# Retention's matrix work dealt out between projection products, output transposes four products later, GpSimd stores by its own queue, and x loaded straight into place

## The chip, the cores and the metric

The kernel runs on one core of one Trainium2 chip. A core has a matrix engine (TensorE, PE in the profile; its weight loads are PEld), a vector engine (VectorE, DVE), a scalar engine (ScalarE, ACT), GpSimd (POOL) and a queue engine (SyncE, SP) that here only issues transfers. Each engine works through its own list of instructions in order; semaphores join the lists. The metric is device microseconds of one launch; lower is better.

## What is computed

One layer of a streaming encoder over 1024 prompt tokens and 64 sample tokens (1088 together), width 1024:

```
xn = rms_norm(x, g_attn)
rq, rk, rv, rg, sq, sk, sv, ga, gb = split(xn @ w_in)          # retention q,k,v,gate; window q,k,v; gates A,B
q, k, v = rope(rq), rope(rk) / 16, rv                          # 4 heads of 256
per head, block by block:   s = (q k^T) * decay;   o = s v + decay * (q state);   state = decay * state + k^T v
A = (rms_norm(o) * silu(rg)) @ w_ret_out
B = window_attention(sq, sk, sv, bias, sinks) @ w_swa_out
x += (sigmoid(ga) * A + sigmoid(gb) * B) @ w_mix_out
x += cross_attention(rms_norm(x), memory);   x += swiglu(rms_norm(x));   y = rms_norm(x)
```

The change concerns the projections `xn @ w_in`, the retention and the way from one to the other. All arithmetic is f32 in accuracy: each operand is split into a high and a low part, and a product is three matrix passes (high x high, high x low, low x high).

## The kernel before, in words

**Products.** Activations lie transposed: features on the 128 partitions, tokens along the row, in two halves of `HALF` = 544 tokens. A projection of 256 output columns (`strassen`) is seven products P1 to P7 instead of eight: P1, P2, P6, P5, P7, P3, P4 in that order. Each product is 24 matrix instructions of 128x272 (4 blocks of features, 2 token quarters, 3 passes; lines 206, 207, 209) from one weight operand `wq` (128x512, high and low) and one activation operand. The activation operands are made once from the quarters of x: B11, B12, B21, B22 (tiles B, b) and the sums T1 to T4 (tiles T). The weight operands are made for every projection: `weight_ops` takes two raw tiles of 128x1024 and forms the seven operands with four sums on GpSimd (lines 184, 185, 187, 190) and, for each operand, `split`: ACT casts the high part (L123), DVE subtracts it for the low part (L124). There is room for five `wq` tiles. Results come out of PSUM, where three pairs of banks (`pq`) are shared, by the scalar engine (u1) and DVE (`u` L263, `stage` L571). The first projection (`values(first, 0, self.plain)`) has eight products and no sums.

**The start.** `start_phase` loads x in 16 pieces of 128x544 into four buffers `xr`, ACT multiplies each by the gain into `xg` (L437), and from `xg` the operands are split; the sums (L1309) follow, all ahead of the key projection of head 0.

**Row norms.** 1/rms is per token and is applied late. `token_squares` loads x again in 16 pieces `xsq`, ACT squares them, DVE adds them up in `rstd` (L463). `token_roots` sums over the partitions on PE (`pt` L472), takes the root (`rsqrt`) and gives `rtok`; `spread_roots` turns it back into a row on all partitions (`pb` L482).

**Order of the projections.** For head h: keys, queries, values, then two columns of the window queries (`w_sq`), then `retention(h)`; after head 3 `w_sk`/`w_sv`, the last `w_sq`, and three sets of gates (`w_ga`, `w_rg`, `w_gb`, four projections each), beside which the memory keys and values are made. `rotated` applies the rotary factors: four multiplications on DVE (L603 to L606) with a table `cs` loaded each time, and a subtraction and an addition on GpSimd (L607, L608); results go to a DRAM buffer `d_qkv` by SP's queue. `project` multiplies by `rstd` (L577, on GpSimd for the window queries) and stores; the window queries go to `d_sq` in 64-token pieces.

**Retention.** Per head four blocks of 256 tokens and the 64 sample tokens. A block loads keys, values and queries (`ks`, `vf`, `qs`) from `d_qkv`, turns keys and values on PE (`pk` L702), splits them, then has three groups of matrix work: scores `pss`, state update `pkv`, output `po`. `ret_out` takes the sums of squares and a copy of `po` on ACT (L816, L817), makes 1/rms by a chain of tiny DVE and ACT operations, scales `ret_o` on ACT (L822), turns it on PE (`pb` L826) and stores it.

**Who sets the order.** The program text is a stream of operations; a scheduler with its own model of time arranges each engine's list, following the text's order as priority and moving work forward where its model sees a gap. `issue_after(x)` holds an operation behind x, and `high_priority` puts it first. `in_order` holds matrix work behind the last matrix instruction issued before. So before the change retention(h) and the projections that follow it in the text are mixed by the scheduler.

Of the kernel before, what the change touches and what calls it, by code (L numbers as in the profile page):

```python
# [41 lines left out]
HC = HALF // 2  # L42
OPS = ("B11", "T1", "T2", "B21", "T3", "B22", "T4", "B12")
# [66 lines left out]
class Kernel:  # L110
    def __init__(self, nc, tc, io, decay):
        self.nc, self.tc, self.io, self.decay = nc, tc, io, decay
        self.later = []
        self.refill = None

# [6 lines left out]
    def split(self, src, hi, lo):  # L122
        self.last_cast = self.nc.scalar.copy(hi, src).ins  # L123
        self.nc.vector.tensor_tensor(out=lo, in0=src, in1=hi.bitcast(F32), op=ALU.subtract)  # L124
# [42 lines left out]
    def weight_ops(self, raws, n=512, skip=()):  # L167
# [13 lines left out]
        tt = nc.gpsimd.tensor_tensor  # L181
# [7 lines left out]
        put("P5", a21)  # L189
        tt(out=a12, in0=a12, in1=a11, op=sub)  # L190
# [21 lines left out]
    def product(self, w, x, name, operand):  # L212
        ps = self.multiply(self.bank_pair(), w[name], x[operand])
        if self.refill is not None:
            self.refill(operand)
        return ps
# [198 lines left out]
    def start_phase(self, ctx):  # L415
# [9 lines left out]
        xr = lambda: sp.tile([P, HALF], F32, tag="xr", bufs=4, name="xr")  # L425
        raws = [self.wp.tile([P, 1024], F32, tag="raw", bufs=2, name="raw") for i in range(2)]

        def columns(j):
            for i in range(2):
                self.load(raws[i][:, j * 512:(j + 1) * 512].rearrange("p (k m) -> p k m", m=P), io["w_v"][i][:, 4 * j:4 * j + 4])  # L430

        def pieces(k0, t):
            hs = slice(t * HALF, (t + 1) * HALF)
            for k in range(k0, k0 + 4):
                x = xr()
                self.load(x, io["xT"][k, :, hs])
                nc.scalar.mul(self.xg[k][:, hs], x, g[:, k:k + 1])  # L437

        for n, (k0, t) in enumerate(((0, 0), (0, 1), (4, 0), (4, 1))):
            pieces(k0, t)  # L440
            if n < 2:
                columns(n)
            if n == 1:
                self.operands_early()
        self.load(self.ident, io["c_ident"])
        w = self.plain_weights(raws)
        self.operands_late()
        self.first_sums()
        self.late_sums()
# [15 lines left out]
    def token_roots(self):  # L465
# [4 lines left out]
        for i in range(9):  # L470
            w = P if i < 8 else SMP
            nc.tensor.matmul(pv[:w, i, :], self.rstd[:, i * P:i * P + w], self.ones[:, :2], start=True, stop=True)  # L472
# [3 lines left out]
    def spread_roots(self):  # L476

        for c0, n in ((0, 512), (512, 512), (1024, SMP)):
            pb = self.norm_psum("pb")
            for a in range(0, n, P):  # L480
                w, i = min(P, n - a), (c0 + a) // P
                self.nc.tensor.matmul(pb[:, a:a + w], self.rtok[:w, i:i + 1].broadcast_to([w, P]), self.ident[:w, :w],  # L482
                                      start=True, stop=True)
# [46 lines left out]
    def bias_table(self):  # L530
# [3 lines left out]
        rb = self.ra.tile([P, 2, BLK], F32, tag="o", bufs=1, name="rb")[:16, 0, :]  # L534
# [5 lines left out]
        nc.vector.tensor_copy(rb, pb[:16, :256])  # L540
        self.store(self.d_rb.rearrange("h (i c) -> h i c", c=256), rb.unsqueeze(1).broadcast_to([16, 64, 256]))
# [8 lines left out]
    def project_phase(self):  # L550
        nc, tc, io = self.nc, self.tc, self.io
        with ExitStack() as ctx:
# [11 lines left out]

            def taken(ps, sb):
                o = stage[count[0] % len(stage)]
                count[0] += 1
# [22 lines left out]
            def rotated(w, h, j):  # L590
# [3 lines left out]
                def emit(i, t, ps, sb):  # L594
# [4 lines left out]
                    cs = self.ra.tile([P, 2, HALF], F32, tag="cs", bufs=1, name="cs")  # L599
                    self.load(cs, io["c_rope"][:, :, half(t)])  # L600
                    ab = self.ra.tile([P, 2, HALF], F32, tag="ab", bufs=1, name="ab")
                    tt = nc.vector.tensor_tensor
                    tt(out=ab[:, 0, :], in0=a, in1=cs[:, 1, :], op=ALU.mult)  # L603
                    tt(out=ab[:, 1, :], in0=b, in1=cs[:, 1, :], op=ALU.mult)
                    tt(out=a, in0=a, in1=cs[:, 0, :], op=ALU.mult)
                    tt(out=b, in0=b, in1=cs[:, 0, :], op=ALU.mult)  # L606
                    nc.gpsimd.tensor_tensor(out=a, in0=a, in1=ab[:, 1, :], op=ALU.subtract)  # L607
                    nc.gpsimd.tensor_tensor(out=b, in0=b, in1=ab[:, 0, :], op=ALU.add)  # L608
                    self.store(self.d_qkv[j, 2 * h, :, half(t)], a)
                    self.store(self.d_qkv[j, 2 * h + 1, :, half(t)], b)  # L610
# [8 lines left out]
            def queries(p):  # L619
                def put(i, t, o):  # L620
                    d = self.d_sq[p, :, :, i, :]
                    r = lambda x: x.rearrange("p (c q) -> p c q", q=64)
                    if t == 0:
                        self.store(d[:, 0:8, :], r(o[:, :512]))
                        self.store(d[:, 8, 0:32], o[:, 512:])
                    else:
                        self.store(d[:, 8, 32:64], o[:, :32])
                        self.store(d[:, 9:17, :], r(o[:, 32:]))
                return put

            values(first, 0, self.plain)
            first = pair("w_k", 0)
            sctx.close()
            stage, count = self.stage_tiles(), [0]
            with ExitStack() as rctx:
                self.ra = rctx.enter_context(tc.tile_pool(name="ra", bufs=1, reuse_waits="tile"))
                for h in range(H):
                    rotated(pair("w_k", h) if h else first, h, 1)
                    if h == 0:
# [1052 lines left out]
```

## Time and profile before

| | us |
|---|---|
| median of 3 runs | 2244.88 (2243.85 to 2248.97) |
| the profiled execution | 2245.5 |
| its span, first to last instruction | 2243.7 |
| PE busy in the span | 2164.6 |
| DVE busy | 1603.1 |
| ACT busy | 883.8 |
| POOL busy | 703.2 |

The profile is one execution; its own time is 0.6 us over the median. Busy is the time in which at least one instruction of an engine is under way; a list of waits names, for each idle stretch of an engine, what ended it. Times in views are microseconds from the first instruction. The columns PEclk and clock are the share of full speed that PE was granted.

### The profile page before, as it was taken

The numbers are of one execution on the slowest core, as the hardware profiler recorded it, in microseconds if no ns is written. First come the engines' busy times: TensorE is split into PE (matmuls) and PEld (weight loads), VectorE is DVE, ScalarE is ACT, GpSimd is POOL, SyncE is SP. The second block draws the span as 40 slices with busy tenths as digits, with TensorE's granted clock in tenths as the row PEclk, the third lists the DMA queues.
The fourth block names the chain that finished last, engine by engine and source line by source line (L and its number), as shares of the span: only waits on it lengthen the run. The fifth ranks groups of instructions, "written<-read, shape, count | busy, mean of one in ns | idle before, by whom it ended". The sixth has DMA issues, their size and how long they took to land.

```text
span 2243.7 us, 42075 instructions
## 1 busy us (share of the span) xinstructions
PE 2164.6 (96%) x16580; PEld 2114.4 (94%) x16580; DVE 1603.1 (71%) x2675; ACT 883.8 (39%) x1902; POOL 703.2 (31%) x471
## 2 busy tenths in 40 slices
PE   7999999999999999999999999999999999999987
PEld 7999998999999987888999998999999999999987
DVE  8986877777687667885455455658777776879777
ACT  7343333345444355554133334333322222335433
POOL 1441533242244112220000000015555565534561
PEclk9999999999999999999999999999999999999999
DMA  5644545443444576326443111422343333376332
GB/s 192 187 134 135 142 138 151 128 137 112 151 145 161 156 227 206 113 82 200 135 153 106 59 48 57 139 88 83 112 140 104 102 107 103 124 248 201 120 119 81
DMA packets 186008, 298.92 MB, mean 133 GB/s; under 512 B 40498, under 2 KB 110034, under 8 KB 185810
## 3 DMA queue, kind: packets, MB, share of 16 engines
q1 hardware_dynamic: 181458, 287.31, 40.9%
q10 hardware_dynamic: 4032, 7.80, 0.9%
q8 instruction: 131, 2.15, 0.4%
q0 software_dynamic: 320, 1.11, 0.1%
q14 instruction: 67, 0.55, 0.1%
HBM read 205.00 MB, written 91.16 MB: 132 GB/s over the span
## 4 chain that ended last, share of the span: by engine, by line
PE 70%; DVE 14%; DMA 7%; issue 3%; POOL 3%; ACT 3%; SPq 0%; POOLq 0%; DVEq 0%; ACTq 0%
PE pq L206 12%; PE pq L209 12%; PE pq L207 12%; PE pd L150 7%; PE pd L152 7%; PE pd L151 7%; DVE wq L124 3%; DVE T L124 1%; DVE B L124 1%; DMA raw<-w_down 1%; PE pss L943 1%; DMA cs<-c_rope 1%; ACT wq L123 1%; DMA hl<-d_op 1%; PE pout L1009 1%
## 5 line engine op out<-in xcount | busy, mean ns | idle before, releaser
L124 DVE TENSOR_TENSOR wq<-raw,wq 128x512 fp32r<-128x512 f32 (+1 forms) x509 | 462.1, 912 | 158.8 <-ACT wq L123 156.6
L123 ACT CAST wq<-raw 128x512 fp32r<-128x512 f32 (+1 forms) x509 | 308.0, 613 | 553.4 <-PE pq L209 206.5
L206 PE MATMUL pq<-T,wq 128*128 128x272 f32 x1832 | 502.8, 292 | 6.8 <-ACT wq L123 5.8
L207 PE MATMUL pq<-T,wq 128*128 128x272 f32 x1832 | 499.0, 289 | 0.0
L206 PE MATMUL pq<-B,wq 128*128 128x272 f32 x1574 | 433.3, 293 | 10.3 <-ACT wq L123 10.2
L207 PE MATMUL pq<-B,wq 128*128 128x272 f32 x1574 | 431.3, 290 | 4.2 <-DVE B L124 4.1
L209 PE MATMUL pq<-T,wq 128*128 128x272 f32 x1832 | 383.3, 289 | 2.5 <-DVE wq L124 2.4
L184 POOL TENSOR_TENSOR raw<-raw 128x512 f32<-128x512 f32 (+1 forms) x59 | 80.8, 1370 | 897.1 <-DVE rs_r L302 487.0
L206 PEld LDWEIGHTS pq<-T,wq 128*128 128x128 f32 x1832 | 346.8, 189 | 8.1 <-ACT wq L123 6.7
L207 PEld LDWEIGHTS pq<-T,wq 128*128 128x128 f32 x1832 | 350.0, 191 | 0.3 <-issue 0.3
L209 PE MATMUL pq<-B,wq 128*128 128x272 f32 x1574 | 329.6, 289 | 0.0
L206 PEld LDWEIGHTS pq<-B,wq 128*128 128x128 f32 x1574 | 298.8, 190 | 11.0 <-ACT wq L123 10.2
L207 PEld LDWEIGHTS pq<-B,wq 128*128 128x128 f32 x1574 | 302.0, 192 | 5.7 <-DVE B L124 5.3
L209 PEld LDWEIGHTS pq<-T,wq 128*128 128x128 f32 x1832 | 286.2, 189 | 3.8 <-DVE wq L124 2.9
L209 PEld LDWEIGHTS pq<-B,wq 128*128 128x128 f32 x1574 | 246.8, 190 | 0.5 <-issue 0.3
L263 DVE TENSOR_TENSOR u<-pq,u 128x544 f32<-128x544 f32 x177 | 127.1, 719 | 76.6 <-PE pq L209 75.9
L187 POOL TENSOR_TENSOR raw<-raw 128x512 f32<-128x512 f32 (+1 forms) x59 | 85.7, 1452 | 120.0 <-DVE wq L124 120.0
L571 DVE TENSOR_TENSOR stage<-pq,u 128x544 f32<-128x544 f32 x112 | 80.3, 717 | 26.0 <-PE pq L209 25.8
L190 POOL TENSOR_TENSOR raw<-raw 128x512 f32<-128x512 f32 (+1 forms) x59 | 90.2, 1529 | 16.0 <-DVE wq L124 12.2
L971 POOL TENSOR_TENSOR t<-t,den 128x768 f32<-128x768 f32 (+2 forms) x34 | 47.6, 1401 | 134.3 <-DVE den L969 56.7
L185 POOL TENSOR_TENSOR raw<-raw 128x512 f32<-128x512 f32 (+1 forms) x59 | 85.5, 1449 | 3.8
L1474 POOL TENSOR_TENSOR y<-u,y 128x544 f32<-128x544 f32 x38 | 61.3, 1628 | 49.3 <-DVE y L1472 24.5
(366 smaller groups left out, 4695.6 us busy)
## 6 DMA issues: line engine op xcount, KB each, us to landing
hl<-d_op SPq DMA_DIRECT2D x84, 272.0 KB, 4.1
d_qkv<-stage SPq DMA_DIRECT2D x44, 272.0 KB, 4.5
d_op<-stage SPq DMA_DIRECT2D x44, 272.0 KB, 2.5
d_op<-ht SPq DMA_DIRECT2D x44, 272.0 KB, 3.8
raw<-w_gate SPq DMA_DIRECT2D x22, 512.0 KB, 3.5
raw<-w_up SPq DMA_DIRECT2D x22, 512.0 KB, 4.2
cs<-c_rope SPq DMA_DIRECT2D x16, 544.0 KB, 4.3
raw<-w_down SPq DMA_DIRECT2D x16, 512.0 KB, 3.9
```

The lines of the kernel that those rows point to most:

```text
L123: self.last_cast = self.nc.scalar.copy(hi, src).ins
L124: self.nc.vector.tensor_tensor(out=lo, in0=src, in1=hi.bitcast(F32), op=ALU.subtract)
L150: mm(ps, wh, xh, start=start, stop=False)
L151: mm(ps, wh, xl, start=False, stop=False)
L152: self.last_mm = mm(ps, wl, xh, start=False, stop=stop).ins
L185: tt(out=a21, in0=a21, in1=a22, op=add)
L187: tt(out=a11, in0=a22, in1=a11, op=sub)
L190: tt(out=a12, in0=a12, in1=a11, op=sub)
L206: mm(ps[:, c, :HC], w[:, 0, ks], x[:, 0, cs], start=start, stop=False)
L207: mm(ps[:, c, :HC], w[:, 0, ks], x[:, 1, cs], start=False, stop=False)
L209: self.last_mm = mm(ps[:, c, :HC], w[:, 1, ks], x[:, 0, c * HC:(c + 1) * HC], start=False, stop=stop).ins
L263: add = lambda out, a, b: nc.vector.tensor_tensor(out=out, in0=a, in1=b, op=ALU.add)
```

## The change

In the words of the code:

- **Start.** The pieces of x are loaded straight into `xg`, all without waiting for a buffer, the first w_v piece behind the first x piece. ACT and DVE apply the gain while they split B11 to B22; then x is scaled in place for the sums, which now stand in a fixed chain (w_k's weights and x's scaling, T2, T1, T3, T4). Twenty matrix instructions on a tile of ones (`warm`) and a tiny ACT instruction stand ahead. The sums of the first w_k weights are on DVE instead of GpSimd.
- **Steps.** `retention` and the row norms become generators. While `self.side` is set, `product` puts each product behind the last matrix instruction, and one step behind each product. The row norms come first: `pt` behind the seventh product of head 0's queries, the spreading behind the third product after that. Retention of head 0 has the 21 products of head 1's queries, values and `w_sq`, and what is left of it is drained at once; heads 1 and 2 have the 28 products of the next head; head 3 has `w_sk`/`w_sv`, the last `w_sq` and the first three `w_ga` projections, which were moved ahead for it.
- **Within a block** the loads for the next block are issued earlier (keys and values behind the scores, queries behind the output), the output adds the state part first, and `ret_out` is cut in two: `ret_scaled` behind `po`, and `ret_turn` (transposes, copy, store) in the next block's state step, four products later.
- **Rotary.** The table `rope` is loaded once; products go into two more `stage` tiles; for heads 0 and 1 the additions are on DVE and stored by SP, for heads 2 and 3 on GpSimd and stored by GpSimd's own queue.
- **Window queries, window keys and values, silu gates** are stored by GpSimd's queue; the window queries are multiplied into long rows of which each is stored with one transfer of 1024 columns and one of 2x32.

The diff, cut to these:

```diff
@@ split, weight_ops, product
+        self.last_low = self.nc.vector.tensor_tensor(out=lo, in0=src, in1=hi.bitcast(F32), op=ALU.subtract).ins
-        tt = nc.gpsimd.tensor_tensor
+        tt = (by or nc.gpsimd).tensor_tensor
-        ps = self.multiply(self.bank_pair(), w[name], x[operand])
+        if self.side is None:
+            ps = self.multiply(self.bank_pair(), w[name], x[operand])
+        else:
+            ps = self.in_order(lambda: self.multiply(self.bank_pair(), w[name], x[operand]))
+            self.in_order(self.step)
@@ start_phase
-                self.load(x, io["xT"][k, :, hs])
-                nc.scalar.mul(self.xg[k][:, hs], x, g[:, k:k + 1])
+        nc.scalar.mul(self.mtok[:, :1], self.ones[:, :1], 1.0)
+        for i in range(WARM):
+            nc.tensor.matmul(warm[:, :P], self.ones, self.ones, start=i == 0, stop=i == WARM - 1)
...
+            self.load(self.xg[k][:, hs], io["xT"][k, :, hs])
...
+            hi = nc.scalar.mul(o[:, 0], src, g).ins
+            return hi, nc.vector.scalar_tensor_tensor(o[:, 1], src, g, o[:, 0].bitcast(F32), ALU.mult, ALU.subtract).ins
...
+            self.second = self.weight_ops(self.load_raws([io["w_k"][i] for i in range(2)]), by=nc.vector)
+            for k in range(4):
+                for b in (b11, b12):
+                    nc.scalar.mul(b, b, g[:, k:k + 1])
+                nc.vector.tensor_tensor(out=b12, in0=b12, in1=b11, op=ALU.subtract)
@@ project_phase
-                    cs = self.ra.tile([P, 2, HALF], F32, tag="cs", bufs=1, name="cs")
-                    self.load(cs, io["c_rope"][:, :, half(t)])
+                    cos, sin = (rope[:, i, half(t)] for i in range(2))
...
+                    add = (nc.vector if h < 2 else nc.gpsimd).tensor_tensor
+                    store = self.store if h < 2 else nc.gpsimd.dma_start
...
+                rotated(first, 0, 1)
+                with tc.issue_after(self.sums_done):
+                    self.token_squares()
+                self.side = self.retention_begin()
+                rotated(pair("w_q", 0), 0, 0)
+                for h in range(1, H):
+                    rotated(pair("w_k", h), h, 1)
+                    if h == 1:
+                        self.finish_side()
+                        self.side = self.retention_steps(0)
+                    rotated(pair("w_q", h), h, 0)
+                    values(pair("w_v", h), h)
+                    queries(pair("w_sq", h - 1), h - 1)
+                    self.finish_side()
+                    self.side = self.retention_steps(h)
+    def step(self):
+        with self.tc.high_priority():
+            return next(self.side, True)
+    def retention_begin(self):
+        for i in range(6):
+            yield
+        self.token_roots()
+        self.retention_setup()
+        for i in range(3):
+            yield
+        self.spread_roots()
+        yield
@@ retention: one step ends at each yield
+            (turn keys and values) yield; (split queries) yield; (scores; load next keys) yield;
+            (state; self.ret_turn(*self.out)) yield; (output; load next queries; self.out = self.ret_scaled(...)) yield
```

How the lists change, at three places. The first is SP's list from the start; `xr` and `xg` are pieces of x, `raw<-w_v` the first weights. Before:

```order
L117 DMA gains<-g_all 128x40
L117 DMA xr<-xT 128x544 x4
L117 DMA raw<-w_v 128x512 x2
L117 DMA xr<-xT 128x544
L117 DMA raw<-w_v 128x512
```

and now:

```order
L119 DMA gains<-g_all 128x40
L119 DMA row<-sinks 1x16
L119 DMA tab<-c_kdec 128x12
L119 DMA tab<-c_gdec 128x12
L119 DMA xg_112<-xT 128x544
L119 DMA raw<-w_v 128x512
L119 DMA xg_112<-xT 128x544
```

Three small tables now stand ahead of x, and the first weights stand behind one piece of x instead of four.

The second is DVE's list at the end of head 0's query projection, up to the last sum of squares (`rstd<-rstd,xsq`) that `pt` on PE waits for. Before:

```order
L606 TENSOR_TENSOR stage_523<-stage_523,cs 128x544
L463 TENSOR_TENSOR rstd<-rstd,xsq 128x544
L124 TENSOR_TENSOR wq<-raw,wq 128x512
L263 TENSOR_TENSOR u_831<-pq,u_829 128x544
L124 TENSOR_TENSOR wq<-raw,wq 128x512
L463 TENSOR_TENSOR rstd<-rstd,xsq 128x544
L263 TENSOR_TENSOR u_830<-pq,u_829 128x544
L571 TENSOR_TENSOR stage_524<-pq,u_831 128x544
```

and now:

```order
L638 TENSOR_TENSOR stage_522<-pq,u_824 128x544
L670 TENSOR_TENSOR stage_521<-stage_521,rope 128x544
L126 TENSOR_TENSOR wq<-raw,wq 128x512 x2
L672 TENSOR_TENSOR stage_521<-stage_521,rope 128x544
L516 TENSOR_TENSOR rstd<-rstd,xsq 128x544
L669 TENSOR_TENSOR stage_522<-stage_522,rope 128x544
L671 TENSOR_TENSOR stage_521<-stage_521,rope 128x544
L675 TENSOR_TENSOR stage_521<-stage_521 128x544
L516 TENSOR_TENSOR rstd<-rstd,xsq 128x544
L672 TENSOR_TENSOR stage_522<-stage_522,rope 128x544
L674 TENSOR_TENSOR stage_521<-stage_521,stage_522 128x544 x2
L516 TENSOR_TENSOR rstd<-rstd,xsq 128x544
```

Now the projection's last results (`stage_522<-pq,u_824`) and nearly all of its rotary work stand ahead of the last sum of squares; before, the last sum stood ahead of them. Counted from the first half of x, 100 DVE instructions led up to it before and 126 do now. On PE `pt` stands in both lists directly behind that projection's seventh product and ahead of the next projection's first.

The third is PE's list where head 0's retention ends (now: the end of head 1's first window queries, where the rest is drained; `pq` is a product). Now:

```order
L154 MATMUL po<-vb,ss 128x256
L816 MATMUL pk<-ident,vf 64x128 x4
L931 MATMUL psss<-qsm,vf 64x64 x2
L975 MATMUL pb<-ident,ret_o 128x128 x4
L940 MATMUL pos<-state,qsm 64x256 x2
L941 MATMUL pos<-kvs,sfs 64x256
L944 MATMUL pkvs<-kvs 128x256 x2
L209 MATMUL pq<-B_172,wq 128x272
```

and before, where the same block's output is turned:

```order
L207 MATMUL pq<-B_217,wq 128x272
L209 MATMUL pq<-B_217,wq 128x272 x2
L826 MATMUL pb<-ident,ret_o 128x128 x2
L702 MATMUL pk<-ident,sf 64x128
L826 MATMUL pb<-ident,ret_o 128x128 x2
L702 MATMUL pk<-ident,sf 64x128
L206 MATMUL pq<-T_274,wq 128x272
```

Before, products stood between the output and its transposes (`pb`); here six small instructions do now. At every other block a transpose now stands four products behind its output. From the first matrix work of the window attention on, PE's list is the same but for places where single groups trade neighbours, and its last 8408 rows are the same word for word.

296 lines of the change are left out of this document (193 added, 103 removed).

## Prediction

> **What bounds the kernel now.** I read the page's busy times first, then the stages, then the list of waits, and then the order of time at the places that the change touches.
>
> ```profile
> span 2243.7 us, 42075 instructions
> PE 2164.6 (96%) x16580; PEld 2114.4 (94%) x16580; DVE 1603.1 (71%) x2675; ACT 883.8 (39%) x1902; POOL 703.2 (31%) x471
> core 0: us, PE busy (x) PEld busy (x) DVE busy (x) ACT busy (x) POOL busy (x), PEclk, DMA share, GB/s
> 0.00:10.20 10.20, 0.00 (x0) 0.00 (x0) 2.16 (x5) 6.13 (x10) 0.20 (x4) 1.00 0.79 244
> 10.20:38.10 27.90, 24.26 (x157) 23.60 (x158) 26.98 (x40) 24.79 (x43) 2.95 (x2) 0.94 0.51 170
> 38.10:86.00 47.90, 47.72 (x376) 47.01 (x374) 45.23 (x60) 22.80 (x39) 19.13 (x11) 1.00 0.67 214
> 86.00:125.60 39.60, 32.40 (x222) 31.69 (x222) 33.75 (x68) 12.86 (x24) 18.80 (x13) 0.87 0.41 124
> 125.60:650.00 524.40, 512.49 (x4031) 501.76 (x4031) 386.58 (x666) 216.01 (x452) 181.22 (x121) 0.99 0.46 138
> 650.00:800.00 150.00, 150.00 (x1212) 150.00 (x1211) 108.34 (x147) 61.95 (x106) 48.93 (x34) 1.00 0.48 154
> 800.00:860.00 60.00, 50.19 (x370) 47.29 (x370) 39.46 (x85) 34.17 (x89) 8.84 (x11) 0.91 0.88 273
> 860.00:2243.00 1383.00, 1347.54 (x10227) 1313.08 (x10223) 960.57 (x1610) 505.12 (x1143) 423.10 (x279) 0.99 0.37 119
> ```
>
> PE bounds the whole: from 650 to 800 us it stands still for nothing, and 1212 instructions in 150 us are 0.124 us each, so a product of 24 takes 3.0 us. Gains can only come from the stretches where PE stands or runs at a lower clock, and those that the change touches lie ahead of 650 us: 10.2 us of nothing, 3.6 us idle with a clock of 0.94 up to 38.1, 7.2 us idle with 0.87 up to 125.6, and 11.9 us idle with 0.99 in the retention of all heads. The waits say what for:
>
> ```profile
> PE pq L206 <- ACT wq L123: 10.2, 1, 10.2
> PE pq L207 <- DVE B L124: 3.6, 3, 1.8
> PE pk L702 <- issue: 2.7, 1, 2.7
> PE pss L150 <- ACT qs L123: 2.2, 1, 2.2
> PE pk L702 <- DMA ks<-d_qkv: 1.9, 1, 1.9
> PE pb L826 <- ACT ret_o L822: 11.3, 7, 4.5
> ```
>
> The first two are the start, the next three the first retention block, and the last is the transpose of the scaled output: seven waits that hold nearly all of the 11.9 us. The change aims at each of these. But from 38 to 86 us DVE is as busy as PE (45.2 of 47.9 us), so what it adds to DVE there needs a price of its own.
>
> **The start, A.** Rows of the start, and of DVE and POOL beside each other:
>
> ```profile
> 1.18 1.84 SPq L117 DMA_DIRECT2D xr<-xT  x4
> 8.87 0.43 SPq L117 DMA_DIRECT2D tab<-c_kdec  x1
> 11.47 0.31 SPq L117 DMA_DIRECT2D row<-sinks  x1
> 4.06 1.28 ACT L437 ACT_TABLE_LOAD   x1 [4.06 <-DMA xr<-xT]
> 5.35 1.39 ACT L437 ACTIVATE xg<-xr,gains 128x544 f32<-128x544 f32 x2
> 9.55 1.13 ACT L123 CAST wq<-raw 128x512 fp32r<-128x512 f32 x2
> 10.22 0.59 PE L206 MATMUL pq<-B,wq 128*128 128x272 f32 x1 [10.22 <-ACT wq L123]
> 10.84 0.43 PE L206 MATMUL pq<-B,wq 128*128 128x272 f32 x1
> 41.64 2.63 DVE L124 TENSOR_TENSOR T<-xg,T 128x544 fp32r<-128x544 f32 x4
> 21.06 0.72 DVE L1309 TENSOR_TENSOR xg<-xg 128x544 f32<-128x544 f32 x1
> 21.70 1.83 DVE L124 TENSOR_TENSOR T<-xg,T 128x544 fp32r<-128x544 f32 x1
> 21.63 1.31 POOL L184 TENSOR_TENSOR raw<-raw 128x512 f32<-128x512 f32 x1 [21.19 <-DMA raw<-w_k]
> 83.67 1.88 DVE L463 TENSOR_TENSOR rstd<-rstd,xsq 128x544 f32<-128x544 f32 x1
> 85.83 2.05 PE L472 MATMUL pt<-ones,rstd 128*128 128x2 f32 x18
> ```
>
> The first x landed 2.9 us after its issue at 1.18. Three small tables now stand ahead of it, at 0.31 to 0.43 us each about 1.2 us, so it lands at 5.3; its gain is one ACT instruction instead of two and the table load is out of the way; the first weight piece comes behind one x piece and its cast takes 0.57 us. The first product starts near 6.9 instead of 10.2, and the 20 warming instructions, even at the 0.43 us of a slow product instruction, fill what was idle (8.6 us at most, which would put it at 9.7). The rest of x and w_v is 5.5 MB; 244 GB/s over 10.2 us, of which 4.06 moved nothing, are some 400 GB/s, hence x is complete about 14 us after 5.3, near 20 us with its last split.
>
> That lead does not last, because of what stands ahead of 1/rms on DVE. DVE's list now has 126 instructions up to the last sum of squares, 20 of them done while x arrives; before it was 100. Of the 26 more, four are the w_k sums and eleven rotary additions (both from GpSimd), the rest rotary products and results that were placed behind it. Four in a row take 2.63 us, 0.635 each with their overlap: 106 x 0.635 = 67.3 us. Then POOL's share: in 38.1 to 86, 60 DVE instructions would be 38.1 us and were busy 45.2, beside 11 of POOL: 0.65 us for each. Eight are left beside them (w_q's and the next w_k's sums): 5.2 us. And DVE now waits for ACT where x is scaled in place: eight instructions at 0.7 us (half of the pair of 1.39) for four subtractions, and again for the first weight casts behind the early copies. No row shows that wait: between 0 and 8 us, taken as 5, since the eight alone are 5.6 against DVE's 2.5. Sum 20 + 67.3 + 5.2 + 5 = 97.5. PE has its 22 products up to there done by 6.9 + 66 = 73 at the earliest, then it stands, since `pt` is next on its list. Before, the last sum began at 83.67 and `pt` ended at 87.9. So at this point the change is 11 us behind (`pt` now takes 1 us).
>
> After it the products of head 1's keys run alone: 21 us, 1 us of spreading, 1.7 us of clock (a long wait's cost by the stretch quoted under B), ending near 122.5. Before, that was 125.6 with 41 instructions of retention already done in between, 5.1 us at 0.124, which now come later: A = 122.5 + 5.1 - 125.6 = **+2 us**. Ends: without POOL's share and ACT's waits -8, with 1.1 us for each POOL instruction (1.83 against 0.72) and 8 of ACT +9.
>
> [...]
>
> **Retention, B.** Idle 11.9 us from 125.6 to 650, and two spells of half clock:
>
> ```profile
> 370.00:420.00 50.00, 42.99 (x322) 42.55 (x321) 43.63 (x69) 19.50 (x44) 19.18 (x12) 0.93 0.44 140
> 373.25 0.39 ACT L816 ACTIVATE ret_o<-po 128x256 f32<-128x256 f32 x1
> 379.67 0.91 ACT L822 ACTIVATE ret_o<-ret_o,rr 128x256 f32<-128x256 f32 x2 [1.31 <-DVE rr L309]
> 380.23 0.63 PE L826 MATMUL pb<-ident,ret_o 128*128 128x128 f32 x2 [4.49 <-ACT ret_o L822]
> 373.74 1.86 DVE L124 TENSOR_TENSOR qs<-qs 128x512 fp32r<-128x512 f32 x1
> 375.52 1.82 DVE L124 TENSOR_TENSOR st<-state,st 128x512 fp32r<-128x512 f32 x1
> 829.84 0.54 POOL L665 DMA_DIRECT2D d_gate<-stage  x1 [1.28 <-ACT stage L580]
> ```
>
> 50 us x 0.07 = 3.5 us of clock, 1.7 for each of its two long waits, so 15.4 us in all. From `po` to the scaled output it takes 7.3 us here; four products are 12, so these waits go. What takes their place is the end of head 0's retention: the 21 products of its round take the loads and 4 x 5 steps, and the sample's steps are drained with no product between `po` and `pb`, about 1 us of small work against that chain. It costs between 0.3 us (the two ACT rows alone, 0.39 and 0.91, less that 1) and 6.3 (the chain of 7.3 less it); I take 4.5, the wait that the same transpose has in the row, and 1.7 us of clock. B = -15.4 + 6.2 = **-9 us**. Ends: -15 with nothing in its place; +7 with new waits in all 16 blocks (below).
>
> **What costs nothing.** The stores moved to POOL's queue issue in 0.54 us each and the rows of 125.6 to 650 leave POOL idle for 343 us; the one thing queued behind them is the next weight sums, which have two projections' room. The rotary table is loaded once instead of 16 times 544 KB, window queries go out in long rows: DMA share 0.46, and PE waits for a DMA only in the 1.9 us row. If that cover failed, `raw` would be late and PE would wait for `wq`. From 650 on the lists are the same but for neighbours, so C = 0, with 2 us either way for what the transfers meet at 800 to 860.
>
> The sum is made against the profiled execution: 2245.5 + 2 - 9 = 2238.5; the median lies 0.6 lower, so **2238 us**.
>
> **Rivals.** First, DVE does not hold PE at 1/rms: the sums of squares come early enough and the start's lead stays. For it speaks that PE ran 38 to 86 us without a gap beside an equally busy DVE; against it the 126 instructions. A = -9, B = -9: 2227. Second, on the other side: the strict order makes PE wait in each block for its own splits. Scores follow the query split by one product, 3.0 us, and from 373.74 two splits alone held DVE for 3.6 us. One microsecond more in each of 16 blocks gives +16: 2254; it decides from 0.45 us a block, where B is -2. Against it: waits for `qs` were 2.2 us once, in the first block alone. Third, both halves fall short: A = +6 and B = -6 leave 2245, no change.
>
> **How the numbers follow.** Likeliest case 0.45 (2230 to 2247), first rival 0.20, second 0.17, third 0.18. A measurement of this kernel tells 0.2%, 4.5 us, from no change, so faster means under 2240.4. Faster: 0.75 of the likeliest and all of the first, 0.54. Slower: the second, 0.05 of the likeliest and 0.1 of the third, 0.21. Same: 0.25. The range takes in the first and most of the second: 2224 to 2254.
>
> **What would show it.** Right: the first product near 7 us; PE idle for some ten microseconds ahead of `pt`, which starts near 97, behind a DVE without gaps; no waits of `pb` but one of about 4.5 us, 21 products and head 0's blocks after 122, near 215; PE idle from 130 to 650 of some 5 us. Wrong: `pt` before 88, which gives the first rival; or waits of `pss` or `po` on `qs`, `ss` in most blocks, which give the second; or waits of `pq` for PSUM from DVE in head 1, which make A larger.

## The result, and the profile after

The changed kernel takes 2261.66 us (median of 5 runs, 2255.13 to 2262.51), the kernel before 2244.88 (5 runs, 2242.14 to 2248.97): a ratio of 1.0063, 95% interval 1.0048 to 1.0079 (that of the two medians is 1.0075). It is slower by 0.63%. The forecast was 2238 us, faster, within 2224 to 2254: both the sign and the range were wrong. The profiled execution took 2262.5 us, 17.0 more than that of before.

First the head of its page, and the same stretches as before (the first now ends at 7.00, where products begin):

```profile
span 2260.7 us, 42155 instructions
PE 2173.5 (96%) x16620; PEld 2121.3 (94%) x16620; DVE 1600.7 (71%) x2696; ACT 879.3 (39%) x1895; POOL 697.7 (31%) x520
core 0: us, PE busy (x) PEld busy (x) DVE busy (x) ACT busy (x) POOL busy (x), PEclk, DMA share, GB/s
7.00:38.10 31.10, 30.27 (x232) 29.23 (x232) 24.50 (x37) 26.03 (x43) 0.00 (x0) 1.00 0.62 225
38.10:86.00 47.90, 38.06 (x259) 36.91 (x258) 44.67 (x66) 19.56 (x34) 6.29 (x5) 0.86 0.51 172
86.00:125.60 39.60, 27.23 (x200) 26.92 (x198) 28.40 (x63) 11.66 (x21) 8.94 (x6) 0.83 0.29 93
125.60:650.00 524.40, 504.65 (x3934) 492.29 (x3933) 375.86 (x669) 210.79 (x445) 184.82 (x159) 0.98 0.38 122
```

The start is better: 232 PE instructions by 38.1 us where there were 157, at full clock. Then it is lost. From 38 to 86 us PE does 259 instead of 376, from 86 to 125.6 us it stands 12.4 us at a clock of 0.83, and from 125.6 to 650, where the waits should have gone, it is idle 19.8 us instead of 11.9. The waits of PE name the places:

```profile
PE pt L525 <- DVE rstd L516: 12.4, 1, 12.4
PE pb L975 <- DVE sf L879: 7.1, 1, 7.1
PE pq L209 <- DVE stage L638: 5.8, 2, 5.4
PE pb L975 <- ACT ret_o L965: 4.9, 1, 4.9
PE pss L152 <- DVE kt L853: 4.8, 4, 1.9
PE pq L209 <- ACT T L125: 3.5, 1, 3.5
PE po L152 <- DVE state L895: 1.8, 3, 0.8
```

The seven waits of `pb` on `ret_o` are one, as forecast; six other kinds are new or larger. To split the loss, I count product instructions on PE in order of time (start and duration in us). In the kernel before, the first one behind head 1's keys, and the 3385th, where the same gates' projections are left in both kernels:

```profile
125.42 0.29 PE L206 MATMUL pq<-B,wq 128*128 128x272 f32 x1
598.40 0.29 PE L206 MATMUL pq<-B,wq 128*128 128x272 f32 x1
```

The same two in the changed kernel:

```profile
131.62 0.29 PE L209 MATMUL pq<-B,wq 128*128 128x272 f32 x1
618.98 0.29 PE L209 MATMUL pq<-B,wq 128*128 128x272 f32 x1
```

At the first of these marks the kernel before has also done 34 matrix instructions of retention, 4.2 us at 0.124 (the prediction counted 41, 5.1 us), but not yet the spreading of 1/rms, 18 instructions of together 2.2 us, which it does at 224 us and the changed kernel ahead of the mark. So A is 6.2 + 4.2 - 2.2 = +8.2 us (forecast +2), B is 20.6 - 8.2 = +12.4 (forecast -9), and the rest of the program gives 3.6 us back (forecast 0 within 2).

**The wait at `pt`.** The stretch in which DVE works up to the last sum of squares (columns as above, DVE is the third pair):

```profile
22.80:104.40 81.60, 59.50 (x427) 58.03 (x426) 74.04 (x107) 38.47 (x66) 12.65 (x8) 0.87 0.41 137
```

In order of time, ACT's first square and the end of `pt`, whose first eight instructions ran at 91.19 (idle time ahead and who ended it in brackets):

```profile
46.31 0.66 ACT L514 ACTIVATE rstd<-xsq 128x544 f32<-128x544 f32 x1 [5.88 <-DMA xsq<-xT]
104.51 0.80 PE L525 MATMUL pt<-ones,rstd 128*128 128x2 f32 x3 [12.37 <-DVE rstd L516]
```

DVE was busy 74.0 of 81.6 us with 107 instructions and ended at 104.4. ACT stood 5.9 us for the first x to be squared, and the casts of the third operand sum (`T`) stood behind it: that is the 3.5 us wait. The load of this x was issued only at 37.69, behind the values' stores and the rotary table of 1.1 MB on SP's list, and landed 8.6 us later.

**The wait at 374 us.** PE waited for `sf`, by which DVE reads the scores out of PSUM; DVE had stood for a `stage` tile that a store had not yet given back, and before that for ACT, and ACT for head 3's query weights. In order of time, backwards, with the issues of that store, of the weights' load and of the bias table's store:

```profile
381.64 0.44 PE L975 MATMUL pb<-ident,ret_o 64*128 64x64 f32 x2 [7.14 <-DVE sf L879]
377.05 0.72 DVE L638 TENSOR_TENSOR stage<-pq,u 128x544 f32<-128x544 f32 x1 [1.95 <-DMA d_sq<-stage]
374.41 0.69 DVE L126 TENSOR_TENSOR wq<-raw,wq 128x512 fp32r<-128x512 f32 x1 [8.04 <-ACT wq L125]
373.76 1.14 ACT L125 CAST wq<-raw 128x512 fp32r<-128x512 f32 x2 [8.97 <-DMA raw<-w_q]
369.67 0.58 POOL L705 DMA_DIRECT2D d_sq<-stage  x1 [9.42 <-issue]
360.18 0.34 SPq L119 DMA_DIRECT2D raw<-w_q  x1
356.32 0.68 POOL L597 DMA_DIRECT2D d_rb<-rb  x1
```

The transfers of these two (last column, us from issue to landing, the median of both loads):

```profile
d_rb<-rb POOLq DMA_DIRECT2D x1, 1024.0 KB, 13.0
raw<-w_q SPq DMA_DIRECT2D x2, 512.0 KB, 12.5
```

And a stretch between, with the share of the transfer engines and GB/s at its end:

```profile
360.00:364.00 4.00, 4.00 (x35) 4.00 (x34) 1.95 (x5) 1.44 (x4) 0.25 (x1) 1.00 0.96 98
```

The bias table's store, 1 MB copied out of 16 partitions, was issued 3.9 us ahead of the weights' load, for which SP had stood 13.5 us until a `raw` tile came free. The store took 13.0 us; in the stretch shown the transfer engines were 0.96 busy and moved 98 GB/s. From 358 to 368 us every packet was one of GpSimd's queue: the loads that SP issued at 360.18, 362.63 and 364.94 moved nothing before 369, and the weights landed 13.5 us after their issue. GpSimd's own next store, of window queries, was issued at 369.67, after 9.4 us in which GpSimd did nothing (what held it the profile does not show; the big store landed at 369.4); it gave DVE's `stage` tile back 1.95 us late. So up to 2 of the 7.1 us came by a store that the change had moved to GpSimd's queue. SP's order of time in the kernel before shows the same 1 MB issued at 351.60, but the second load of these weights already at 340.92:

```profile
340.92 0.35 SPq L117 DMA_DIRECT2D raw<-w_q  x1
351.60 0.67 SPq L120 DMA_DIRECT2D d_rb<-rb  x1
```

### The profile page after: what moved, and what is told of

Same layout as the page of the kernel before. It is cut to its first block, busy times and chain, and to the rows that moved or that the text cites. A ratio compares the mean times of both kernels' runs of the same rounds, so it can differ in the third digit from the quotient of the medians.

```text
span 2260.7 us, 42155 instructions
## 1 busy us (share of the span) xinstructions
PE 2173.5 (96%) x16620; PEld 2121.3 (94%) x16620; DVE 1600.7 (71%) x2696; ACT 879.3 (39%) x1895; POOL 697.7 (31%) x520
## 4 chain that ended last, share of the span: by engine, by line
PE 73%; DVE 12%; DMA 7%; issue 3%; POOL 2%; ACT 2%; SPq 0%; DVEq 0%; ACTq 0%; POOLq 0%
PE pq L209 14%; PE pq L212 14%; PE pq L210 13%; PE pd L152 7%; PE pd L153 7%; PE pd L154 7%; DVE wq L126 3%; PE pss L1093 1%; DVE T L126 1%; DMA raw<-w_down 1%; DMA hl<-d_op 1%; PE pout L1159 1%; DMA qs<-d_qkv 1%; DVE stage L638 1%; DVE B L126 1%
## 5 line engine op out<-in xcount | busy, mean ns | idle before, releaser
L209 PE MATMUL pq<-B,wq 128*128 128x272 f32 x1526 | 420.4, 293 | 0.9 <-DVE stage L638 0.5
L210 PE MATMUL pq<-B,wq 128*128 128x272 f32 x1526 | 416.0, 289 | 1.9 <-DVE B L126 1.9
L186 POOL TENSOR_TENSOR raw<-raw 128x512 f32<-128x512 f32 (+1 forms) x58 | 80.4, 1385 | 971.9 <-DVE rs_r L309 487.6
L209 PEld LDWEIGHTS pq<-T,wq 128*128 128x128 f32 x1832 | 348.0, 190 | 20.6 <-ACT wq L125 7.0
L212 PE MATMUL pq<-B,wq 128*128 128x272 f32 x1526 | 317.0, 288 | 0.0
L210 PEld LDWEIGHTS pq<-B,wq 128*128 128x128 f32 x1526 | 292.3, 192 | 2.6 <-DVE B L126 2.6
L209 PEld LDWEIGHTS pq<-B,wq 128*128 128x128 f32 x1526 | 289.5, 190 | 2.3 <-DVE stage L638 0.7
L212 PEld LDWEIGHTS pq<-B,wq 128*128 128x128 f32 x1526 | 238.2, 189 | 0.0
L189 POOL TENSOR_TENSOR raw<-raw 128x512 f32<-128x512 f32 (+1 forms) x58 | 82.7, 1426 | 111.8 <-DVE wq L126 111.8
L193 POOL TENSOR_TENSOR raw<-raw 128x512 f32<-128x512 f32 (+1 forms) x58 | 85.8, 1480 | 15.7 <-DVE wq L126 12.2
L1121 POOL TENSOR_TENSOR t<-t,den 128x768 f32<-128x768 f32 (+2 forms) x34 | 48.0, 1410 | 131.6 <-DVE den L1119 55.8
L187 POOL TENSOR_TENSOR raw<-raw 128x512 f32<-128x512 f32 (+1 forms) x58 | 85.1, 1467 | 3.7
```

Of the source, the lines that this page charges most:

```text
L187: tt(out=a21, in0=a21, in1=a22, op=add)
L209: mm(ps[:, c, :HC], w[:, 0, ks], x[:, 0, cs], start=start, stop=False)
L210: mm(ps[:, c, :HC], w[:, 0, ks], x[:, 1, cs], start=False, stop=False)
L212: self.last_mm = mm(ps[:, c, :HC], w[:, 1, ks], x[:, 0, c * HC:(c + 1) * HC], start=False, stop=stop).ins
```

## The experiments

Times are medians; each ratio is to the kernel before on the same chip, with its 95% interval. "Less than the changed kernel" is a difference of medians that were taken on different chips. By the ratios the first three edits below bring 9, 7 and 21 us of 2245, each within some 4 us, where the medians say 11.0, 9.4 and 22.8.

### 1/rms four products later

```diff
 def retention_begin(self):
-    for i in range(6):
+    for i in range(10):
         yield
     self.token_roots()
```

> The changed kernel with 1/rms four products later on PE (`pt` behind the 26th product instead of the 22nd). Theory: DVE's list up to the last sum of squares ends at 104 us whatever PE does, and PE stands before `pt` only because nothing else is next on its list; then the wait of 12.4 us at 91.9 goes, and with it the 2.7 us that its half clock costs behind it (5.5 us of the spell of 13.65 lie behind the wait): 15 us less than the changed kernel, about 2247, ratio to the kernel before near 1.001. Rival: DVE bounds this stretch, and PE meets the same delay at its next need of it (PSUM not emptied, the weight splits of head 1's keys, `kt` of the first block): no more than 5 us less, 2257 or above, with waits of `pq` or `pk` on DVE between 92 and 140 us.

Measured: 2250.67 us, 1.0023 (1.0014 to 1.0033), 11.0 us less than the changed kernel. PE's waits from 85 to 140 us:

```profile
PE pb L536 <- DVE rtok L312: 1.9, 1, 1.9
PE pt L525 <- DVE rstd L516: 1.6, 1, 1.6
```

The last sum began at 103.8 us, as in the changed kernel (103.7); DVE's list did not move, PE had other work. The theory holds: by products counted PE is 10.8 us ahead of the changed kernel behind head 1's keys, and 3.5 us of small waits at these two steps are about the rest of its 15.

### The bias table's store elsewhere, in four

```diff
 def retention_steps(self, h):
     yield from self.retention(h)
-    if h == 1:
-        yield
-        self.bias_table()
     if h == H - 1:
 ...
         self.ret_turn(*self.out)
+        yield
+        yield from self.bias_table()
 ...
 def bias_table(self):
 ...
-    nc.gpsimd.dma_start(self.d_rb..., rb.unsqueeze(1).broadcast_to([16, 32, 512]))
 ...
+    for i in range(4):
+        yield
+        nc.gpsimd.dma_start(self.d_rb...[:, 8 * i:8 * i + 8], rb.unsqueeze(1).broadcast_to([16, 8, 512]))
```

> The changed kernel with the bias table made in head 3's round instead of at the end of head 1's, and its store of 1 MB cut into four of 256 KB, one product apart. Theory: the store holds all 16 DMA engines for 13 us (share 0.96 at 97 GB/s from 358 to 370 us), so that the query weights of head 3 land 13.5 us after their issue, and ACT, DVE and PE wait in a row for them: the wait of 7.1 us at 374 goes, with 2.5 us of clock behind it: 10 us less than the changed kernel, about 2252, ratio 1.003; weights land within 5 us of their issue at that place. Rival: that wait comes from the sample's output or from the PSUM bank that the scores hold, whose order on PE and DVE is the same here: it stays within 1 us, and the time within 3 us of the changed kernel's 2262; or the four stores only hold another load, of the gates' weights, and the wait turns up between 480 and 570 us.

Measured: 2252.26 us, 1.0032 (1.0021 to 1.0043), 9.4 us less. In the same place the weights now land in 5.4 us (13.5 and 11.5 in the changed kernel):

```profile
raw<-w_q SPq DMA_DIRECT2D x2, 512.0 KB, 5.4
```

Among PE's waits from 125 to 650 us none of `pb` on `sf` is left; the drain and the small waits are as they were. The edit moves the store and cuts it up; which of the two is needed it does not tell.

```profile
PE pss L152 <- DVE kt L855: 5.0, 4, 2.0
PE pb L977 <- ACT ret_o L967: 4.9, 1, 4.9
```

### No drain between heads

```diff
-    self.finish_side()
-    self.side = self.retention_steps(h)
+    self.side = chain(self.side, self.retention_steps(h))
```

> The changed kernel with the steps of one head's retention going on in the next head's products, where the changed kernel runs what is left with no product between. Theory: at 220 to 233 us the drain costs 0.6 + 0.4 + 4.9 us of waits and 4.3 us of half clock behind them, 10 us; all of it goes: about 2252, ratio 1.003. Rival: all later heads' steps come four products later and meet other neighbours on DVE, so that the small waits of `pss` and `po` on `kt` and the state (6.6 us in seven places now) grow by as much: no more than 4 us less.

Measured: 2238.89 us, 0.9969 (0.9957 to 0.9981): 22.8 us less, more than twice what either theory gave. PE's waits from 125 to 650 us (the first two; the third is 0.2):

```profile
PE pss L153 <- DVE kt L853: 3.5, 2, 2.6
PE po L153 <- DVE state L895: 3.1, 2, 2.5
```

The loads of head 3's query weights, how long they took and when SP issued them:

```profile
raw<-w_q SPq DMA_DIRECT2D x2, 512.0 KB, 3.5
```

```profile
344.67 0.35 SPq L120 DMA_DIRECT2D raw<-w_q  x1
352.11 0.35 SPq L120 DMA_DIRECT2D raw<-w_q  x1
```

The drain is gone, and with it the wait at 374: the store of 1 MB, here issued at 355.25, took 12.3 us as ever, but both loads were ahead of it. So this edit removed two things, 10.2 us of drain and 9.6 us of store (7.1 and 2.5 of clock), and the small waits are 6.8 us with nothing of clock instead of 8.3. That makes 21.3 us; by products counted up to the gates it is 21.2 us ahead of the changed kernel. To see whether the store's place still matters, this edit and late roots alone:

> Late roots and no drain, the bias table and its store of 1 MB as in the changed kernel. Theory: the store costs only by the loads that are issued behind it and needed within its 13 us; with the steps going on, head 3's query weights are loaded ahead of it, so that its place no longer matters: the ratio of the three edits together, 0.9935, within 0.001, with no wait of PE over 3 us between 350 and 385 us. Rival: the 1 MB costs PE its wait wherever the loads stand: 9 us more, ratio 0.9975, with that wait back.

Measured: 2232.49 us, 0.9936 (0.9917 to 0.9956); the only wait of PE from 350 to 385 us is 2.0 for `kt`. So the store costs by what is issued behind it and needed soon; a cost of its own, if there is one, is below the 4 us that this run can tell.

### The three together

> The edits of the first three runs together: 1/rms four products later, the bias table in head 3's round with its store in four, and one head's steps going on in the next head's products. Theory: each removes its own wait. Late roots brought 11.0 us against the changed kernel, no drain 22.8, and in that run the wait for the query weights of head 3 was gone too, as their load was issued 11 us and 3 us ahead of the store, so that the 9.4 us of the late store are in the 22.8 already: 2261.7 - 33.8 = 2228, ratio 0.9925. Rival: the waits are one and the same lateness of DVE that moves on, and the gains don't add: no lower than 2238, the best so far.

Measured: 2229.57 us, 0.9935 (0.9924 to 0.9947), 1.6 us from the sum: faster than both kernels. PE's waits from 125 to 650 us:

```profile
PE po L153 <- DVE state L897: 2.8, 1, 2.8
PE pss L153 <- DVE kt L855: 1.2, 2, 0.6
```

And the two stretches that had lost most:

```profile
86.00:125.60 39.60, 36.20 (x275) 35.67 (x274) 38.11 (x76) 13.53 (x24) 12.27 (x8) 0.96 0.31 95
125.60:650.00 524.40, 520.15 (x4124) 510.64 (x4123) 392.42 (x692) 220.97 (x465) 204.51 (x178) 1.00 0.42 132
```

With these, PE is idle 4.3 us in the stretch that held 11.9 before, at full clock. Counted by products as above, B is -11.5 us with the three edits (the marks lie at 122.77 and 586.22). Without the 4.0 us of small waits that are left it would be -15.5, where the prediction took -15.4 for the waits that go.

### Work of no use in the wait

```diff
+    for i in range(50):
+        self.last_mm = nc.tensor.matmul(idle[:, :P], self.ones, self.ones, ...).ins
     ps = self.norm_psum("pt")
```

> The changed kernel with 50 matmuls of ones by ones ahead of `pt`, about 11 us of work that nobody reads, in the wait of 12.4 us. Theory: the clock is halved because PE stands; then the spell of 13.65 us from 96 us is gone or no longer than 3.4, `pt` still starts near 104, and the products behind it run at full clock: 2.5 us less than the changed kernel, about 2259. Rival: the clock falls for what the other engines or the transfers do, or by a budget of work: the spell stays, and the time is the same or up to 3 us more, since half-speed matmuls of no use end behind the last sum of squares.

Measured: 2260.91 us, 1.0065 (1.0050 to 1.0080): no gain. The spell shrank from 13.65 us to 3.41, so the clock followed PE's idling here. But the dummies ended 2.8 us before the last sum, and that rest halved the clock again where work was waiting. The stretches behind `pt` of this kernel:

```profile
105.00:108.00 3.00, 3.00 (x16) 2.97 (x16) 1.88 (x21) 0.30 (x2) 0.00 (x0) 0.56 0.38 122
108.00:111.00 3.00, 3.00 (x23) 3.00 (x23) 1.25 (x9) 1.13 (x2) 0.00 (x0) 0.87 0.16 52
```

And of the changed one:

```profile
105.00:108.00 3.00, 3.00 (x15) 2.97 (x16) 1.15 (x11) 0.30 (x2) 0.00 (x0) 0.50 0.53 182
108.00:111.00 3.00, 3.00 (x19) 3.00 (x19) 1.46 (x18) 0.00 (x0) 0.00 (x0) 0.68 0.10 19
```

Five instructions more in six microseconds: 0.6 us, which the measurement can't tell.

### The rotary additions on GpSimd

```diff
-    add = (nc.vector if h < 2 else nc.gpsimd).tensor_tensor
+    add = nc.gpsimd.tensor_tensor
```

> The changed kernel with the rotary additions of heads 0 and 1 on GpSimd, as those of heads 2 and 3 are: eight fewer instructions on DVE ahead of the last sum of squares. Theory: DVE's list holds `pt`, so eight times 0.635 us less bring `pt` from 104.4 to 99.3, and the time to 2256.5. Rival: GpSimd and DVE hold each other off where both read SBUF, as the 1.83 us beside a GpSimd sum shows: each of the eight costs DVE as much as it saves, `pt` stays within 1 us of 104, and the time within 2 us of 2262.

Measured: 2265.76 us, 1.0100 (1.0084 to 1.0115). The rival holds for `pt`: the last sum began at 102.5 instead of 103.7. DVE in the same stretch as above:

```profile
22.80:104.40 81.60, 60.18 (x440) 59.00 (x438) 74.93 (x99) 38.36 (x65) 25.08 (x15) 0.88 0.42 138
```

Eight instructions fewer (seven additions, and a multiplication that now stands behind the sum), and DVE as long busy: 99 take 0.757 us each where 107 took 0.692, that is 6.4 us more for seven more of GpSimd, 0.9 us for each. By products counted it is 0.7 us ahead of the changed kernel behind head 1's keys and 4.0 behind it two projections later. Between these lies a new wait, where head 1's additions now are on GpSimd too (PE's waits from 125 to 210 us):

```profile
PE pss L152 <- DVE kt L853: 3.5, 2, 3.2
```

### The squares behind the casts

On late roots:

```diff
-    with tc.issue_after(self.sums_done):
+    with tc.issue_after(self.sums_done), tc.issue_after(self.casts_done):
         self.token_squares()
```

> Late roots, and the first four squares of x on ACT behind the casts of the last operand sums instead of ahead of the third's. Theory: at 40 to 46 us ACT stands 5.9 us for x to be squared, with the third sums' casts behind it, and PE waits 3.0 us for these: against late roots alone the wait goes with its half clock, 2 to 3 us each, but the fourth sums on DVE end near 62 as before, so that the wait there takes some of it back: 2248, 3 us less than late roots. Rival: the squares, begun later, end later by as much as 10 us, and the wait at `pt`, 1.6 us in late roots, grows to as much: 2254 or more.

Measured: 2254.69 us, 1.0052 (1.0039 to 1.0064), 4 us more than late roots. The rival holds: the wait for the cast fell to 0.4 us, but the last sum came at 109.1. PE's waits from 30 to 140 us:

```profile
PE pt L525 <- DVE rstd L516: 6.8, 1, 6.8
PE pq L209 <- DVE stage L638: 4.9, 1, 4.9
PE pq L209 <- DVE u L270: 2.3, 1, 2.3
```

The wait near 58 us stays in all kernels with this start: DVE has the fourth operand sums (54 to 61 us in the changed kernel) ahead of the results that PE's PSUM waits for. On the three edits, the first two weight casts ahead of ACT's scalings:

```diff
     put("P2", a12)
+    self.two = self.last_cast
 ...
+with tc.issue_after(self.two):
     for k in range(4):
         b11, b12 = qs[k][:2]
         for b in (b11, b12):
             nc.scalar.mul(b, b, g[:, k:k + 1])
```

> The three edits together, and on ACT the first two casts of head 0's key weights ahead of the eight scalings of x, as DVE stands 22.8 to 27.7 us mostly for these casts. Theory: DVE's list starts 3 us earlier and with it the operand sums: the waits at 47 and 60 us shrink by as much: 2226.5. Rival: DVE's order has the differences of x, which need the scalings, ahead of the weights' low parts, so it only waits for the other: 2229.6 within 1.5 us, or more.

Measured: 2230.27 us, 0.9931 (0.9918 to 0.9943), the same as without it; the wait near 58 us is 5.6. How it could be had shorter stays open.

### No warming, and the old start

```diff
-    warm = self.norm_psum("warm")
-    for i in range(WARM):
-        nc.tensor.matmul(warm[:, :P], self.ones, self.ones, start=i == 0, stop=i == WARM - 1)
```

> The changed kernel without the 20 warming matmuls. Theory: they take PE's slow first 3 us off the first products (28 of their 40 passes ran at 0.11 us, the first 12 at 0.21), worth 1.5 us at 30 us, and nothing at the end, since DVE's list sets `pt`: first product at 7.2 still, `pt` at 104, time the same within 1.5 us. Rival: at a halved clock the first products fall behind x, spells of half clock follow each other up to 40 us, and the stretch behind gets longer: 2265.

Measured: 2263.42 us, 1.0084 (1.0070 to 1.0097), 1.8 us above the changed kernel with intervals that overlap. The second instruction of the first product, without warming:

```profile
7.52 0.43 PE L210 MATMUL pq<-B,w 128*128 128x272 f32 x1
```

And with it, in the changed kernel:

```profile
7.38 0.29 PE L210 MATMUL pq<-B,w 128*128 128x272 f32 x1
```

By products counted, the kernel without warming is 2.2 us behind the changed one at head 1's keys and level with it at the end of these two traces. That is near the 1.5 us of the theory at the start; that the warming is worth anything in all is not shown.

The start of the kernel before, on the three edits:

```diff
 def start_phase(self, ctx):
-        self.load(self.xg[k][:, hs], io["xT"][k, :, hs])
+            x = xr()
+            self.load(x, io["xT"][k, :, hs])
+            nc.scalar.mul(self.xg[k][:, hs], x, g[:, k:k + 1])
 ...
+    w = self.plain_weights(raws)
+    self.operands_late()
+    self.first_sums()
+    self.late_sums()
 ...
-first = self.second
+first = pair("w_k", 0)
```

> The three edits together (2229.6 us), and the start of the kernel before in place of the new one: x scaled by ACT into its place, weights split plainly, operand sums made from it, no warming matmuls, the first key weights' sums on GpSimd. The steps, the merged rotary table and the stores stay. Theory: the new start begins 3 us earlier, but its sums on DVE come later, and PE stands 8 us at 47 and 60 us for them with 5 us of half clock; the old start has no such wait, so head 0's queries end near 88 instead of 92 and head 1's keys near 113 instead of 123: 2220, ratio 0.989. Rival: the new start is no worse than the old, as the waits only move with DVE's list, and the first product at 10.2 instead of 7.2 and the gaps that the old start had ahead of 38 us, 3.6 us, come back: 2232 or more.

Measured: 2236.94 us, 0.9959 (0.9947 to 0.9972), where the three edits have 0.9935. My theory fell: the old start is no better. The first product behind head 1's keys begins at 121.5 us with it and at 122.8 with the new one; at the gates it is 2.3 us behind, and 4.6 us more between 765 us and 1504 us, where the edit touches nothing, with a spell of half clock at 1030 us (the granted clock is 0.99 from 860 to 1100 us, and 1.00 with the three edits). So the new start is not the loss; by the ratios the old one costs some 5 us, of which only the 2.3 lie where the edit works, and what the new start is worth by itself stays open.

### The stores back on SP

On the three edits:

```diff
-    store = self.store if h < 2 else nc.gpsimd.dma_start
+    store = self.store
```

(and so for the window queries, keys and values and the retention gate)

> The three edits together, and the stores of GpSimd's results issued by SP instead of GpSimd's own queue (rotated heads 2 and 3, window queries, window keys and values, the retention gate). Theory: the queue costs nothing either way, since PE waits for a DMA nowhere between 130 and 650 us once the bias table's store is out of the way: 2229.6 within 2 us. Rival: SP issues in order, so a store that waits for GpSimd keeps the weight and head loads behind it, which land late: waits of `pq` for `wq` or of `pk` for `ks` of a few microseconds each, 2235 or more.

Measured: 2227.10 us, 0.9915 (0.9902 to 0.9929). The queue costs nothing here, where the big store is out of the way (in the changed kernel a store on it had its part in the wait at 374 us); if anything SP is better, by an amount at the edge of the two intervals. This is the fastest version, 0.85% under the kernel before.

## Why the prediction was wrong, step by step

**A, the start.** The mechanism was right: the first product at 7.15 us, DVE without large gaps, PE standing before `pt`. The step that failed is the sum for DVE's list, 97.5 us, which came to 104.4. Its terms, by the stretch shown above: x was split by 22.8 instead of 20 (2.8 us); DVE was busy 74.0 us where 67.3 + 5.2 were taken (1.5); it stood 7.6 us where 5 were taken for waits on ACT (2.6). And PE was not at `pt` by 73 but by 91, as it had waited 3.5 and 5.4 us for operand sums and PSUM with half clock behind each; this cost nothing more, since `pt` came later still. Behind it the clock cost 2.7 us, not 1.7, and the spreading took 2.2, not 1: 6.9 + 1.0 + 1.2 is the 9.1 us by which the next product came later, at 131.6 instead of 122.5. A is off by less, 6.2, since two readings erred the other way: 34 instructions of retention had been done before, not 41, and the spreading of the kernel before, which lies in B's stretch, was left out. The "eleven rotary additions" were seven; eleven is what came from GpSimd with the four sums, and the count of 126 stands. The late roots show that the 12.4 us were not forced by DVE's list but by the place of a step: four products later they shrink to 1.6.

The price of GpSimd beside DVE, 0.65 us for each of its instructions, was too low for the additions of the run that puts them on GpSimd: they cost DVE 0.9 us each, less than the 1.1 of the upper end. For the eight of the changed kernel it was near: DVE was busy 1.5 us longer than with 0.65, and 2.1 us shorter than with 1.1. In the changed kernel's trace a weight split of DVE (`wq`, 128x512, both inputs in SBUF) took 0.68 us alone and 1.24 with an operation of GpSimd under way (medians of 306 and 198); `u`, which reads a product from PSUM, took 0.72 in both cases (102 and 75).

**B, retention.** The 11.9 us of idling and the spells behind them did go, as the three edits together show, and the -15.4 was right in size. Three things in their place: the drain (forecast 4.5 + 1.7, measured 0.6 + 0.4 + 4.9 of waits and 4.3 of half clock, 10.2); small waits in the blocks (forecast none; 4.8 for `kt` and 1.8 for the state, with 1.7 of clock 8.3); and the store of 1 MB (9.6), which had no term at all. -15.4 + 10.2 + 8.3 + 9.6 = +12.7; counted by products it is +12.4. The step that failed most is "What costs nothing": the prediction named what would show if the cover failed, `raw` late and PE waiting, but looked at DMA shares over 500 us, 0.46, and not at what stands ahead of each weights' load at the one place where 1 MB leaves, nor at the stores that stand behind each other on GpSimd's queue. With the store and A as measured, no other error was needed for the wrong sign: 8.2 - 9 + 9.6 is +8.8.

On that store: the row shows 98 GB/s with the transfer engines 0.96 busy, all of it this store; from 372 to 376 us they moved 349 GB/s at 1.00. Why the store is so slow no run shows; a table spread over more partitions was not tried.

**C.** 0 within 2 was too narrow: 3.6 us came back. By products counted the changed kernel is 20.6 us late up to 795 us and 17.4 late behind the window attention, where PE's waits came to 8.0 us instead of 11.0. Why they are shorter was not tried.

**The rivals.** The first (no hold at `pt`) was wrong by 12.4 us. The second came about at a half of its size, 8.3 us of 16, and not by its cause: PE waited in seven places for the keys turned (`kt`) and for the state, not for the query splits. The third, A = +6 and B = -6, had A's direction; none had a B above zero from a cause other than the blocks' own waits.

## What to carry to other kernels

When an order is written out by hand, set each step by the engine that finishes its input, counted to the end of that engine's list, and not by the products that lie between; here a step too early cost its whole wait of 12.4 us, the same step four products later 1.6. Look at what is issued behind every large store within the time that it holds the transfer engines (13.0 us for the 1 MB here): PE waited for the load behind it. Let a side chain run on across the boundary of its round: the drain, with no product between its steps, cost 10.2 us here.

## What the hardware showed that I had not expected

A wait costs more than itself, by the clock: in the changed kernel a wait of 1.9 us brought a spell of 3.4 us at half clock, waits of 3.5 to 7.1 us 6.8 to 10.2, and that of 12.4 us 13.7, part of it within the wait. Not every short wait does: one of 1.6 us at 400 us brought none. Filling the wait with idle matmuls held the clock at 1.00 from 92 us until they ended, and earned nothing that could be measured. Moving seven additions from DVE to an engine that was 85% idle left DVE's busy time where it was (74.9 us, 74.0 with them). And one store of 1 MB out of 16 partitions, on GpSimd's queue, left SP's loads without a packet for some ten microseconds, from 358 to 368 us.
